# Gate and up products with both parts of x in one matmul of 512 columns, and weight sums made ahead

## The chip, the cores and the metric

One core of a Trainium2 chip runs the whole layer. The metric is the device time of one execution in microseconds (us), as the median of the runs given. A profile of one further execution stands beside it, with the granted clock of the matrix engine.

The engines are named as in the profile: PE multiplies matrices (PEld loads its weights), DVE and ACT do elementwise work, POOL and SP mostly issue DMAs. Each engine takes its own instructions strictly in the order of the program and waits for the others by semaphores.

## The reference

One encoder layer over x of 512 tokens by 2048, all in float32:

```
h = rmsnorm(x, attn_norm_w);  P = h @ w_in            # 2048 -> 6176 columns
attn = three-dilation windowed attention on P         # 16 heads of 64
gla  = bidirectional gated linear attention on P      # 4 heads
x = x + concat(attn, gla) @ w_out                     # 2048 -> 2048
h = rmsnorm(x, ffn_norm_w)
x = x + (silu(h @ w_gate) * (h @ w_up)) @ w_down      # 2048 -> 5632 -> 2048
out = rmsnorm(x, final_norm_w)
```

## The kernel before

**Precision.** A float32 operand f is used as two parts: hi, which ACT makes by casting f to the matrix engine's rounded format (fp32r), and lo = f - hi, which DVE makes. A product is the sum of three matmuls, hi by hi, hi by lo and lo by hi, which add up in PSUM. So each product costs one ACT cast and one DVE subtraction for each operand, and three PE instructions, each with a weight load of its own.

**PSUM and SBUF.** PSUM is eight banks of 512 columns (`ps`). SBUF is cut by hand into 70 slots of 512 columns (`s2`, tiles a) and 16 slots of 1024 columns (`s4`, tiles b). A slot is taken from the front of a queue and put back at its end. Whoever takes a slot waits until the last user of what stood there is through, so the order in which slots are put back decides who waits for whom. The order on every engine is the order in which this Python program emits its instructions.

**The projections.** `jobs` is a list of 24 products that `run_job` (L263) runs in turn; the first 16 are columns of w_in (twelve jobs, here by number: 0 qk0, 1 av0, 2 qk1, 3 qk2, 4 av1, 5 qk3, 6 gqk0, 7 gv0, 8 gqk1, 9 gv1, 10 gr0, 11 gr1) and four column blocks of w_out (12 to 15, out0 to out3). A job is 16 halves; a half is 128 rows of weights by 512 columns and 12 matmuls of 512 columns (L285 to L287 or L293 to L295). `Stream` (L155) loads pieces of two halves through SP, three pieces held at most, and casts and subtracts three halves ahead of use (L196, L197). After each half `run_side` runs some steps of attention or GLA, which go on in between: one step has matmuls and transposes on PE, and elementwise work that the next step's PE work needs. The evacuation of a w_out block makes the inputs of gate/up (`evac_out`, L998): transposed, weighted, and split by `pair_operands`.

**Gate and up.** The product of a 2048-row block and 256 columns of w_gate or w_up (a unit) is done by a scheme with 7 products in place of 8: with rows and columns each cut in two, R are the raw blocks and Z sums of blocks on the weight side, B and T the like on the x side. There are 44 units (22 blocks, gate and up in turn); each has four pieces of 512 rows (`seq`), and a piece two pairs p. So a piece has 2 x 7 products, and before the change 42 matmuls of 256 columns (L1147 to L1149). For a piece the kernel
- loads 512 KB through SP (`load`, L1069 on, three held at most),
- makes the four sums Z on DVE (`sums`, L1089 to L1091: one instruction of 512 columns and two of 256),
- casts (ACT, L1101: 768 columns of R, 1024 of Z) and subtracts (DVE, L1106) one piece ahead of PE (`split`),
- runs the products (`products`), which add up in four banks for a unit.

Two units fill PSUM: one is added to while the other is read. After the fourth piece `evac` (L1153) is queued in `urgent`, and one of its steps runs after each piece of the next unit (three steps for each of the first eight pieces): DVE adds the seven products into four result blocks, reading the banks themselves. Then `finish` (L1179): for a gate unit, two DVE multiplications by the row scale and a Silu on ACT; for an up unit, one DVE multiplication by the gate, and a store through POOL to `gd` in DRAM, from where the down product reads.

**After gate and up** come four small jobs of w_down, the class `Down` with the same seven-product scheme, and the final norm.

Of the kernel before, what the change touches and what calls it, by code (L numbers as in the profile page):

```python
# [117 lines left out]
def layer(nc, tc, x, attn_norm_w, w_in, rel_table, gw_f, gb_f, gw_b, gb_b, gla_norm_w, w_out,  # L118
# [7 lines left out]
    with tc.manual_schedule(), \  # L126
# [25 lines left out]
        state = {"credit": 0.0, "set": None}  # L152
# [96 lines left out]
        class Job:  # L249
            drop = None  # L250

# [11 lines left out]
        def run_job(j):  # L263
# [6 lines left out]
            for i in range(j.n):  # L270
# [690 lines left out]
        def half_split(src, n=512):  # L961

            if n == 512:
                hi, lo = s2.get(F32R), s2.get(F32R)
                return (hi, lo), hi.t, lo.t, hi.f
            o = s2.get(F32R, [P, 2, 256])
            return (o,), o.t[:, 0], o.t[:, 1], o.f[:, 0]

        def pair_operands(q, fs_):
# [10 lines left out]
            todo = []  # L980
            slots = []
            for src, n in ((f1.t[:, a], 256), (f2.t, 512), (t13.t, 512), (t24.t, 512)):
                sl, hi, lo, hf = half_split(src, n)
                slots += sl
                todo.append((src, hi, lo, hf))
            for i in range(4):
                src, hi, lo, hf = todo[i]
                act.copy(hi, src)
                sub(lo, src, hf)
                put((f1, f2, t13, t24)[i])  # L990
                if i % 2:
                    yield
            (_, b1h, b1l, _), (_, f2h, f2l, _), (_, t13h, t13l, _), (_, t24h, t24l, _) = todo
            xs[q] = dict(slots=slots, B11=(b1h, b1l), B21=(f2h[:, a], f2l[:, a]), B22=(f2h[:, z], f2l[:, z]),
                         T1=(t13h[:, a], t13l[:, a]), T3=(t13h[:, z], t13l[:, z]),
                         T2=(t24h[:, a], t24l[:, a]), T4=(t24h[:, z], t24l[:, z]))
# [62 lines left out]
        class Blocks:  # L1059
# [9 lines left out]
            def load(self):  # L1069
                while self.n_load < self.n and len(self.raw) < 3 and s4.free:  # L1070
                    w, k, n_kt, col, n = self.source(*self.seq[self.n_load])
                    r = s4.get(F32, self.shape(4))
                    sp.dma_start(out=r.t.rearrange("p a b c -> p (a b c)").rearrange("p (k c) -> p k c", k=n_kt),
                                 in_=w[k * P:(k + n_kt) * P, col:col + n].rearrange("(k p) c -> p k c", p=P))
                    self.raw[self.n_load] = r
                    self.n_load += 1

# [34 lines left out]
        class Feed(Blocks):  # L1112
# [3 lines left out]

            def __init__(self):
# [4 lines left out]
                self.begin(seq, 2, P)  # L1122

# [3 lines left out]

            def products(self, i, banks):
                st_ = self.sets.pop(i)
                piece = self.seq[i][1]  # L1130
                first, last = piece == 0, piece == self.per - 1
                a, z = slice(0, 256), slice(256, 512)
                A, B, C, E = (b.t for b in banks)
                for p in range(2):
                    q = 2 * piece + p
                    (rh, rl), (sh, sl) = st_
                    R = lambda n: (rh.t[:, p, n], rl.t[:, p, n])
                    Z = lambda n: (sh.t[:, p, n], sl.t[:, p, n])
                    x_ = xs[q]
                    prods = [(A[:, a], R(0), x_["B11"], True), (A[:, z], R(2), x_["B21"], False),  # L1140
                             (B[:, a], Z(2), x_["T2"], True), (C[:, a], Z(1), x_["T1"], True),
                             (C[:, z], Z(0), x_["T3"], False), (E[:, a], Z(3), x_["B22"], True),
                             (E[:, z], R(1), x_["T4"], False)]
                    for o, (wh, wl), (xh, xl), head in prods:
                        head = head and first and p == 0
                        end = last and p == 1
                        mm(o, wh, xh, start=head, stop=False, skip_group_check=True)  # L1147
                        mm(o, wh, xl, start=False, stop=False, skip_group_check=True)  # L1148
                        mm(o, wl, xh, start=False, stop=end, skip_group_check=True)  # L1149
# [3 lines left out]
            def evac(self, u, banks):  # L1153
# [4 lines left out]
                add = lambda o, x_, y_: dve.tensor_tensor(o, x_, y_, op=OP.add)  # L1158
                c_ = s4.get(F32, [P, 2, 512])
                c = c_.t.rearrange("p f t -> p (f t)")  # L1160
                A, B, C, E = (b.t for b in banks)
                t1, t2 = s2.get(), s2.get()
                act.copy(t1.t[:, a], A[:, a])
                add(c[:, a], A[:, z], t1.t[:, a])
                put(banks[0])
                dve.tensor_tensor(t1.t[:, z], t1.t[:, a], B[:, a], op=OP.subtract)
                yield
                add(t2.t.rearrange("p (h t) -> p h t", h=2), C.rearrange("p (h t) -> p h t", h=2),
# [112 lines left out]
        def drop_g(k):  # L1281
            put(*gT.pop(k))
# [321 lines left out]
```

## Time and profile before

| what | us |
|---|---|
| median of 3 runs | 2239.39 (2237.67 to 2239.72) |
| profiled execution, its own time | 2238.72 |
| its span in the trace | 2236.9 |
| projections of w_in with attention and GLA | 9 to 680 |
| projection of w_out | 680 to 868 |
| gate and up (first and last of its matmuls) | 868 to 1762 |
| down product and end | 1762 to 2237 |

The granted clock of PE was 0.997 over the span. A row of groups in the trace reads: line, engine, operation, what is written and what is read, shapes, count | busy time in us, mean ns of one | idle time of the engine just before them, and what ended it. A row of windows has for each stretch its length and the busy time of PE, PEld, DVE, ACT and POOL (with counts of instructions), then the granted clock, the share of time in which the 16 DMA engines were busy, and what they moved in GB/s. A row of the timeline is start, duration, engine, line. The end of a matmul is modelled: how fast matmuls follow each other is read from their starts.

### The profile page before, as it was taken

The numbers are of one execution on the slowest core, as the hardware profiler recorded it, in microseconds if no ns is written. First come the engines' busy times: TensorE is split into PE (matmuls) and PEld (weight loads), VectorE is DVE, ScalarE is ACT, GpSimd is POOL, SyncE is SP. The second block draws the span as 40 slices with busy tenths as digits, with TensorE's granted clock in tenths as the row PEclk, the third lists the DMA queues.
The fourth block names the chain that finished last, engine by engine and source line by source line (L and its number), as shares of the span: only waits on it lengthen the run. The fifth ranks groups of instructions, "written<-read, shape, count | busy, mean of one in ns | idle before, by whom it ended". The sixth has DMA issues, their size and how long they took to land.

```text
span 2236.9 us, 37003 instructions
## 1 busy us (share of the span) xinstructions
PE 2210.6 (99%) x14814; PEld 2037.6 (91%) x14814; DVE 1635.0 (73%) x2717; ACT 1002.4 (45%) x1637; POOL 115.8 (5%) x173
## 2 busy tenths in 40 slices
PE   8999999999999999999999999999999999999998
PEld 7888887888888888999999999999999999999986
DVE  4366665745454446988888888888888788888877
ACT  5344444444444344444433444344433555555542
POOL 0000000000000100000000000000000110022220
PEclk9999999999999999999999999999999999999999
DMA  5525625232324432334333333333333865688992
GB/s 205 158 75 146 181 81 142 83 123 66 95 64 143 138 125 68 113 114 124 116 123 121 114 123 114 114 123 114 123 115 116 256 179 179 171 190 185 241 368 76
DMA packets 211805, 307.78 MB, mean 138 GB/s; under 512 B 15376, under 2 KB 131264, under 8 KB 211633
## 3 DMA queue, kind: packets, MB, share of 16 engines
q1 hardware_dynamic: 192480, 259.37, 36.8%
q0 software_dynamic: 18256, 44.99, 8.5%
q8 instruction: 116, 1.90, 0.4%
q10 hardware_dynamic: 896, 1.06, 0.1%
q14 instruction: 57, 0.46, 0.1%
HBM read 246.58 MB, written 46.20 MB: 131 GB/s over the span
## 4 chain that ended last, share of the span: by engine, by line
PE 88%; issue 6%; POOL 2%; DMA 1%; DVE 1%; ACT 1%; SPq 0%; POOLq 0%; ACTq 0%; DVEq 0%
PE ps L1149 13%; PE ps L1148 13%; PE ps L1147 13%; PE ps L294 6%; PE ps L295 6%; PE ps L293 6%; PE ps L285 5%; PE ps L286 5%; PE ps L287 5%; PE ps L1376 2%; PE ps L1375 2%; PE ps L1374 2%; POOL md L1396 2%; PE ps L514 1%; PE ps L841 1%
## 5 line engine op out<-in xcount | busy, mean ns | idle before, releaser
L1149 PE MATMUL ps<-a,b 128*128 128x256 f32 x2464 | 697.7, 283 | 2.9 <-DVE b L1106 2.9
L1147 PE MATMUL ps<-a,b 128*128 128x256 f32 x2464 | 697.5, 283 | 0.0
L1148 PE MATMUL ps<-a,b 128*128 128x256 f32 x2464 | 697.3, 283 | 0.0
L1101 ACT CAST b<-b 128x768 fp32r<-128x768 f32 x480 | 445.5, 942 | 537.5 <-DVE b L1106 284.8
L1106 DVE TENSOR_TENSOR b<-b,b 128x768 fp32r<-128x768 f32 x480 | 510.2, 1089 | 139.2 <-PE ps L1148 62.5
L1149 PEld LDWEIGHTS ps<-a,b 128*128 128x128 f32 x2464 | 473.0, 192 | 3.7 <-DVE b L1106 3.7
L1148 PEld LDWEIGHTS ps<-a,b 128*128 128x128 f32 x2464 | 473.0, 192 | 0.0
L1147 PEld LDWEIGHTS ps<-a,b 128*128 128x128 f32 x2464 | 473.0, 192 | 0.0
L197 DVE TENSOR_TENSOR a<-b,a 128x512 fp32r<-128x512 f32 x292 | 195.0, 686 | 125.5 <-ACT a L196 122.8
L1376 PE MATMUL ps<-b,a 128*128 128x256 f32 x896 | 254.5, 284 | 3.6 <-DVE a L1339 3.6
L1374 PE MATMUL ps<-b,a 128*128 128x256 f32 x896 | 254.4, 284 | 1.5 <-ACT a L1338 1.5
L1375 PE MATMUL ps<-b,a 128*128 128x256 f32 x896 | 254.2, 284 | 0.0
L196 ACT CAST a<-b 128x512 fp32r<-128x512 f32 x292 | 171.3, 617 | 51.5 <-DMA b<-in_w_in_dram 18.2
L294 PE MATMUL ps<-a,a 128*128 128x512 f32 x464 | 182.0, 392 | 2.3 <-DVE a L197 2.1
L293 PE MATMUL ps<-a,a 128*128 128x512 f32 x464 | 184.1, 397 | 0.0
L295 PE MATMUL ps<-a,a 128*128 128x512 f32 x464 | 181.6, 391 | 0.0
L1376 PEld LDWEIGHTS ps<-b,a 128*128 128x128 f32 x896 | 172.7, 193 | 4.0 <-DVE a L1339 4.0
L1374 PEld LDWEIGHTS ps<-b,a 128*128 128x128 f32 x896 | 172.7, 193 | 1.7 <-ACT a L1338 1.7
L1375 PEld LDWEIGHTS ps<-b,a 128*128 128x128 f32 x896 | 172.8, 193 | 0.0
L1089 DVE TENSOR_TENSOR b<-b 128x512 f32<-128x512 f32 x240 | 164.0, 684 | 7.1 <-DMA b<-in_w_up_dram 4.1
L285 PE MATMUL ps<-a,a 128*128 128x512 f32 x416 | 168.2, 404 | 0.0
L286 PE MATMUL ps<-a,a 128*128 128x512 f32 x416 | 163.3, 392 | 0.0
(224 smaller groups left out, 3071.6 us busy)
## 6 DMA issues: line engine op xcount, KB each, us to landing
b<-in_w_gate_dram SPq DMA_DIRECT2D x88, 512.0 KB, 3.5
b<-in_w_up_dram SPq DMA_DIRECT2D x88, 512.0 KB, 3.6
b<-in_w_down_dram SPq DMA_DIRECT2D x88, 512.0 KB, 5.3
b<-in_w_in_dram SPq DMA_DIRECT2D x96, 256.0 KB, 4.5
b<-in_w_in_dram SPq DMA_DIRECT2D x48, 512.0 KB, 4.0
b<-in_w_out_dram SPq DMA_DIRECT2D x32, 512.0 KB, 4.4
md<-a POOLq DMA_DIRECT2D x56, 256.0 KB, 8.5
a<-a SPq DMA_DIRECT2D x96, 128.0 KB, 2.3
```

The lines of the kernel that those rows point to most:

```text
L285: mm(o, wh.t[:, c], xh.t, start=first, stop=False)
L293: mm(o, xh.t[:, c], wh.t[:, w], start=first, stop=False)
L294: mm(o, xh.t[:, c], wl.t[:, w], start=False, stop=False)
L295: mm(o, xl.t[:, c], wh.t[:, w], start=False, stop=last)
L1101: act.copy(hi.t, src)
L1106: dve.tensor_tensor(lo.t, src, hi.f, op=OP.subtract)
L1147: mm(o, wh, xh, start=head, stop=False, skip_group_check=True)
L1148: mm(o, wh, xl, start=False, stop=False, skip_group_check=True)
L1149: mm(o, wl, xh, start=False, stop=end, skip_group_check=True)
L1374: mm(o, xh[:, t], wh, start=first and h == 0, stop=False, skip_group_check=True)
L1375: mm(o, xh[:, t], wl, start=False, stop=False, skip_group_check=True)
L1376: mm(o, xl[:, t], wh, start=False, stop=last, skip_group_check=True)
```

## The change

It has four parts, all for gate and up.

1. **Products.** The two parts of an x operand now lie side by side in one slot of 2 x 256 columns. From unit 2 on, hi of the weights is multiplied with both parts by one matmul of 512 columns into a bank of its own, and lo of the weights with hi of x by one of 256 columns into that bank's first half. The products run product by product (both pairs of one, then the next) instead of pair by pair. Units 0 and 1 keep the three matmuls of 256 columns and four banks.
2. **Evacuation.** A unit holds seven banks. After its last piece `leave` copies all of them to SBUF on ACT, which sets the banks free; the steps of `evac` then work on the copies, and first fold the two halves of each (DVE, 256 columns).
3. **Weight sums ahead.** For 110 of the 176 pieces (all with q of 0 or 2, and q of 3 for gate units) the sums are made during jobs 1 to 14 by the generator `ahead`: SP loads the 512 KB piece, DVE makes four sums in place (four instructions of 256 columns), POOL stores the 512 KB to `sd` in DRAM. A step is one sum; `run_job` takes 1.3 steps after each half of jobs 1 to 5, 2.3 in jobs 6 to 11 and 2.9 in jobs 12 to 14. In gate and up SP then loads such a piece's sums beside its raw weights.
4. **Splits of x.** `pair_operands` makes seven casts and subtractions of 256 columns in place of one of 256 and three of 512.

```diff
@@ run_job
+                state["ahead"] += j.ahead
+                while state["ahead"] >= 1:
+                    state["ahead"] -= 1
+                    next(state["sums"], None)
             j.evac(banks)
@@ pair_operands
+            xs[q] = {}
+            for n, (name, f, h) in enumerate((("B11", f1, a), ("B21", f2, a), ("B22", f2, z), ("T1", t13, a),
+                                              ("T3", t13, z), ("T2", t24, a), ("T4", t24, z))):
+                o = xs[q][name] = s2.get(F32R, [P, 2, 256])
+                act.copy(o.t[:, 0], f.t[:, h])
+                sub(o.t[:, 1], f.t[:, h], o.f[:, 0])
...
@@ class Feed
+            PRODUCTS = (("R", 0, "B11"), ("R", 2, "B21"), ("Z", 2, "T2"), ("Z", 1, "T1"), ("Z", 0, "T3"),
+                        ("Z", 3, "B22"), ("R", 1, "T4"))
...
+                self.pre = {i: n for n, i in enumerate(i for i, (u, q) in enumerate(seq) if q != 1 and (q < 3 or u % 2 == 0))}
+                self.sd = dr.tile([len(self.pre), P, 1024], F32, name="sd")
...
+            def ahead(self):
+                todo, held = deque(self.pre), deque()
+                def load():
+                    if todo and len(held) < 2 and len(s4.free) > 1:
+                        r = s4.get(F32, self.shape(4))
+                        self.fetch(todo[0], r)
+                        held.append((todo.popleft(), r))
+                load()
+                yield
+                while todo or held:
+                    load()
+                    if not held:
+                        yield
+                        continue
+                    i, r = held.popleft()
+                    b = lambda n: r.t[:, :, n]
+                    for o, x_ in ((1, 0), (0, 2), (2, 1), (3, 2)):
+                        dve.tensor_tensor(b(o), b(o), b(x_), op=OP.add)
+                        yield
+                    pool.dma_start(out=self.sd[self.pre[i]], in_=r.t.rearrange("p a b c -> p (a b c)"))
+                    put(r)
...
+                    if i in self.pre:
+                        S = self.S[i] = s4.get(F32, self.shape(4))
+                        sp.dma_start(out=S.t.rearrange("p a b c -> p (a b c)"), in_=self.sd[self.pre[i]])
...
+            def sums(self, i):
+                if i in self.pre and i == self.n_sums:
+                    self.n_sums += 1
+                else:
+                    Blocks.sums(self, i)
@@ products
-                    for o, (wh, wl), (xh, xl), head in prods:
-                        mm(o, wh, xh, start=head, stop=False, skip_group_check=True)
-                        mm(o, wh, xl, start=False, stop=False, skip_group_check=True)
-                        mm(o, wl, xh, start=False, stop=end, skip_group_check=True)
...
+                for n, (side_, b, x) in enumerate(self.PRODUCTS):
+                    for p in range(2):
...
+                        if u > 1:
+                            o = banks[n].t
+                            mm(o, wh, x_.rearrange("p s t -> p (s t)"), start=head, stop=False, **kw)
+                            mm(o[:, 0:256], wl, xh, start=False, stop=end, **kw)
...
+            def leave(self, u, banks):
+                out_ = []
+                for n, b in enumerate(banks):
+                    e = s2.get()
+                    c = slice(0, 256 if u < 2 and n == 1 else 512)
+                    act.copy(e.t[:, c], b.t[:, c])
+                    put(b)
+                    out_.append(e)
+                return out_
@@ evac (the steps, from unit 2 on)
+                    fold = lambda *ns: [add(m[n], m[n], es[n].t[:, z]) for n in ns]
...
+                fold(0, 1, 2)
+                add(c[:, a], m[1], m[0])
+                dve.tensor_tensor(m[0], m[0], m[2], op=OP.subtract)
+                yield
+                fold(3, 4)
+                add(m[3], m[3], m[0])
+                add(c[:, 768:1024], m[3], m[4])
+                add(m[4], m[4], m[0])
+                yield
+                fold(5, 6)
+                add(c[:, 256:512], m[5], m[3])
+                add(c[:, 512:768], m[6], m[4])
+                put(*es)
+                yield
                 self.finish(u, c_, c)
@@ run
-                        banks[u] = [ps.get() for _ in range(4)]
+                        banks[u] = [ps.get() for _ in range(7 if u > 1 else 4)]
...
                     if q == self.per - 1:
-                        urgent.append(self.evac(u, banks.pop(u)))
+                        urgent.append(self.evac(u, self.leave(u, banks.pop(u))))
@@ at the end
+        state["sums"] = ff.ahead()
+        for n, j in enumerate(jobs[1:15]):
+            j.ahead = 1.3 if n < 5 else 2.3 if n < 11 else 2.9
```

More of the change, by code (lines that the diff above doesn't have):

```diff
@@ L979, in pair_operands @@
             yield
[L980 to L991, printed above, removed]
+            xs[q] = {}
[4 more added lines that the diff above has]
+                sub(o.t[:, 1], f.t[:, h], o.f[:, 0])
+                if n in (0, 2, 4, 6):
+                    put(f)
+                if n in (2, 6):
                     yield
[L993 to L996, printed above, removed]
         def evac_out(c):
@@ L1134, in products @@
[L1134 to L1143, printed above, removed]
-                    for o, (wh, wl), (xh, xl), head in prods:
[L1145 to L1149, printed above, removed]
+                (rh, rl), (sh, sl) = st_
@@ L1573, in layer @@
             if n == n_out:
+                assert next(state["sums"], None) is None
                 ff.run()
```

77 lines of the change are left out of this document (47 added, 30 removed).

## The prediction

> **What bounds the kernel now.** I read the page first: the shares of the engines and the chain of work that ended last.
>
> ```profile
> PE 2210.6 (99%) x14814; PEld 2037.6 (91%) x14814; DVE 1635.0 (73%) x2717; ACT 1002.4 (45%) x1637; POOL 115.8 (5%) x173
> DMA  5525625232324432334333333333333865688992
> GB/s 205 158 75 146 181 81 142 83 123 66 95 64 143 138 125 68 113 114 124 116 123 121 114 123 114 114 123 114 123 115 116 256 179 179 171 190 185 241 368 76
> PE 88%; issue 6%; POOL 2%; DMA 1%; DVE 1%; ACT 1%; SPq 0%; POOLq 0%; ACTq 0%; DVEq 0%
> ```
>
> PE works 99% of the span and holds 88% of the chain: what PE no longer does is won, as long as nothing else becomes late. Next come the windows by stage (job 1, jobs 2 and 3, jobs 7 and 8, out0 to out2, and all of gate/up).
>
> ```profile
> 64.50:108.02 43.52, 43.52 (x194) 36.04 (x192) 14.40 (x24) 10.71 (x20) 0.00 (x0) 1.00 0.69 203
> 108.00:228.00 120.00, 119.81 (x613) 100.39 (x612) 79.23 (x175) 57.15 (x124) 0.00 (x0) 1.00 0.38 106
> 410.30:468.70 58.40, 58.33 (x300) 48.97 (x299) 34.72 (x75) 25.55 (x54) 0.00 (x0) 1.00 0.44 134
> 468.70:522.50 53.80, 53.80 (x251) 45.12 (x250) 23.82 (x43) 22.43 (x52) 1.07 (x2) 1.00 0.26 79
> 680.20:727.20 47.00, 46.92 (x210) 38.55 (x209) 23.78 (x43) 23.14 (x51) 2.13 (x4) 1.00 0.44 146
> 727.20:774.20 47.00, 47.00 (x217) 39.08 (x217) 19.69 (x36) 17.55 (x36) 4.29 (x8) 1.00 0.40 134
> 774.20:821.20 47.00, 47.00 (x217) 39.11 (x216) 19.69 (x36) 17.86 (x36) 4.30 (x8) 1.00 0.41 135
> 868.15:1761.90 893.75, 890.82 (x7418) 889.96 (x7417) 776.86 (x1178) 370.87 (x446) 12.79 (x24) 1.00 0.39 121
> ```
>
> PE is full in all of them, at the full granted clock. DVE is busy 87% of gate/up (776.86 of 893.75), but only 33 to 66% before it. So the change takes work from PE where PE is the bound, and puts DVE and DMA work where these have room. The sum is made from what PE wins, less what each of these moves gives back.
>
> **Part 1, the matmuls.** Each matmul carries a weight load, and a short one costs more per column than a long one. The starts show it, where gate/up begins and ends:
>
> ```profile
> 868.15 0.39 PE L295 MATMUL ps<-a,b 128*128 128x512 f32 x1
> 868.38 0.28 PE L1147 MATMUL ps<-a,b 128*128 128x256 f32 x1
> 868.49 0.28 PE L1148 MATMUL ps<-a,b 128*128 128x256 f32 x1
> 868.61 0.28 PE L1149 MATMUL ps<-a,b 128*128 128x256 f32 x1
> ...
> 1761.87 0.28 PE L1149 MATMUL ps<-a,b 128*128 128x256 f32 x1
> 1761.99 0.40 PE L293 MATMUL ps<-a,a 128*128 128x512 f32 x1
> ```
>
> A matmul of 512 columns followed by one of 256 takes 0.23 us (868.15 to 868.38), and one of 256 takes 0.12 whether 256 or 512 follow (1761.87 to 1761.99). More exactly, by windows: job 1 has 192 weight loads in 43.52 us, 226.7 ns each; gate/up has 7418 matmuls in 890.82 busy us, 120.1 ns each. So 256 further columns cost 106.6 ns, and 13.5 ns come with each matmul. Three of 256 take 360.3 ns, one of 512 and one of 256 take 346.8. From unit 2 on there are 42 units x 4 pieces x 14 = 2352 such triples: 2352 x 13.5 ns = 31.8 us. Bounds: the starts at 868 leave the short one after a long one 0.11 to 0.12 us, so a pair takes 340 to 349 ns and the gain is 27 to 47 us. I take -32: it is the mean over thousands of rows.
>
> The Trainium skill, "TensorE: Matmul & The Clock Gate", section "Back-to-back issue gap", gives a warm gap of N / 2.4 + 2.5 ns, that is, only 2.5 ns that come with each matmul. By it 2352 fewer matmuls would win an estimated 6 us. The 13.5 ns of the windows above speak against it for matmuls that each load weights; what would follow is a rival below.
>
> **Part 2, does DVE or ACT become the bound of gate/up?**
>
> ```profile
> L1106 DVE TENSOR_TENSOR b<-b,b 128x1024 fp32r<-128x1024 f32 x240 | 293.3, 1222 | 17.7 <-PE ps L1148 8.5 <-ACT b L1101 6.3 <-PE ps L1376 2.9
> L1101 ACT CAST b<-b 128x1024 fp32r<-128x1024 f32 x240 | 251.9, 1049 | 222.9 <-PE ps L1148 116.5 <-PE ps L1376 55.9 <-DVE b L1106 36.0
> L1106 DVE TENSOR_TENSOR b<-b,b 128x768 fp32r<-128x768 f32 x240 | 229.3, 955 | 121.5 <-PE ps L1148 54.0 <-ACT b L1101 25.6 <-PE ps L1149 19.2
> L1101 ACT CAST b<-b 128x768 fp32r<-128x768 f32 x240 | 200.4, 835 | 314.5 <-DVE b L1106 248.8 <-PE ps L1376 24.7 <-DMA gd<-b 19.2
> L1089 DVE TENSOR_TENSOR b<-b 128x512 f32<-128x512 f32 x240 | 164.0, 684 | 7.1 <-DMA b<-in_w_up_dram 4.1 <-DMA b<-in_w_down_dram 3.0
> L1090 DVE TENSOR_TENSOR b<-b,b 128x256 f32<-128x256 f32 x240 | 102.0, 425 | 8.3
> L1158 DVE TENSOR_TENSOR a<-ps,a 128x512 f32<-128x512 f32 x44 | 30.1, 684 | 0.0
> L1184 DVE TENSOR_TENSOR b<-b,a 128x512 f32<-128x512 f32 x44 | 28.3, 684 | 0.0
> L1188 DVE TENSOR_TENSOR b<-b,b 128x1024 f32<-128x1024 f32 x22 | 26.8, 1217 | 0.0
> L1185 ACT ACTIVATE b<-b 128x1024 f32<-128x1024 f32 x22 | 23.3, 1061 | 115.8 <-DVE b L1184 110.6 <-PE ps L1149 5.2
> L1393 ACT COPY a<-ps 128x512 f32<-128x512 f32 x72 | 40.0, 589 | 14.6 <-PE ps L1376 11.6
> ```
>
> For a unit DVE now has 4 x (1222 + 955) for the splits, 4 x (684 + 2 x 425) for the sums, three adds of 256 and two of 512 columns for the evacuation (2.64 us) and 1.29 us of finishing (two of 684 or one of 1217): 18.8 us against 168 matmuls = 20.2 us. After the change the sums fall to 1.5 pieces per unit (66 of 176 over 44), and the evacuation is 14 adds of 256 columns, 425 each: 8.7 + 2.3 + 5.95 + 1.3 = 18.2 us against PE's 4 x 14 x 0.3468 = 19.4. The ratio stays, 94 for 93%, so DVE isn't the bound. ACT has 4 x (1049 + 835) + 7 x 589 + 1061 / 2 = 12.2 of 19.4 us.
>
> What does change is a queue. ACT takes the seven copies of `leave` in order, and the casts two pieces ahead stand behind them; for a gate unit a Silu stands in front of them, which waits for DVE (110.6 us of L1185's idle time is that). Take T as the start of an up unit's last piece. The casts of the next piece wait for slots that PE sets free at T (116.5 us of L1101's idle time): cast 1.05 and subtraction 1.22 end at T + 2.3, the two multiplications at T + 3.6, the Silu at T + 4.7, the first copy at T + 5.3. PE fills the spare bank first and needs the copied one at T + 4.85 (a piece) + 0.69 (one product) = T + 5.54: in time by 0.2 us. The other copies follow at 0.5 to 0.6 us, faster than the 0.69 at which PE asks, and end at T + 8.5. Then cast 0.84 and subtraction 0.96 end at T + 10.3, but PE wants that part of lo at T + 9.7 + 0.23: 0.3 to 0.4 us late, once for each gate unit's finish. 21 x 0.3 = 6 us. Bounds: 0 if the copies overlap a little more, and 1.5 us each, 32 us, if DVE is an evacuation step and a sum late when the multiplications are due. I take +6.
>
> The second DMA of a piece has its time: 6.5 loads and half a store of 512 KB in 19.4 us in place of 4 and a half in 20.2 is a share of about 0.39 x 7 / 4.5 x 20.2 / 19.4 = 0.63, with loads two and more pieces ahead (9.7 us; they land in 3.5).
>
> **Part 3, the sums made ahead.** The program order puts 19 to 22 of the 440 adds into each of jobs 1 to 5, 34 to 41 into each of jobs 6 to 11, and 45, 48 and 24 into out0 to out2. At 0.425 us each DVE rises from 66 to 81% in jobs 2 and 3 (79.23 + 41 x 0.425 = 96.7 of 120), from 59 to 89% in job 7 (34.72 + 41 x 0.425 = 52.1 of 58.4), and from 51 to 91% in out0 (23.78 + 19.1 of 47). What covers them is DVE's own idle time:
>
> ```profile
> L566 DVE CUSTOM_DVE_ANT_0 a<-ps,b 128x512 f32<-128x512 f32 x64 | 44.2, 691 | 49.2 <-PE ps L554 49.0
> L197 DVE TENSOR_TENSOR a<-b,a 128x512 fp32r<-128x512 f32 x292 | 195.0, 686 | 125.5 <-ACT a L196 122.8 <-DMA a<-in_x_dram 1.0 <-DMA b<-in_w_in_dram 1.0
> ```
>
> In attention DVE waits 0.77 us for PE in each of 64 steps (L566) and 0.43 for the cast before each split (L197); 1.3 adds are 0.55 us. In jobs 6 to 11 the step is longer, and 0.98 us of adds per half go into 1.5 to 1.9 us free (jobs 7 and 8, the stretch less DVE's busy time, over 16 halves). Steps with more of their own work than the mean will make PE wait here and there: 0 to 20 us over eleven jobs, and I take +4. If an add waits for its load, the splits and all of attention's or GLA's work queue behind it on DVE; PE has three halves (3 x 43.52 / 16 = 8 us) of split weights in hand.
>
> DMA is tighter. A piece moves 1.05 MB (load and store).
>
> ```profile
> q1 hardware_dynamic: 192480, 259.37, 36.8%
> q0 software_dynamic: 18256, 44.99, 8.5%
> b<-in_w_gate_dram SPq DMA_DIRECT2D x88, 512.0 KB, 3.5
> b<-in_w_out_dram SPq DMA_DIRECT2D x32, 512.0 KB, 4.4
> gd<-b POOLq DMA_DIRECT2D x22, 512.0 KB, 3.2
> ```
>
> Cheapest, at the 368 GB/s of the busiest slice (over 90% busy), it takes all 16 engines 2.85 us. Dearest, at the mean of the queues, 0.524 MB at 315 GB/s (259.37 MB in 36.8% of 2236.9) and 0.524 at 237 (44.99 in 8.5%), it takes 3.9. out0 and out1 carry 0.44 x 47 + 0.40 x 47 = 39.5 us now and get 12 + 11 pieces: 105 us at the cheap price, 129 at the dear one, in 94. So these two jobs become bound by DMA: +11 to +35 us, less the 8 us that PE has in hand once. The store is one run of 4 KB per partition, like `gd`'s, which lands fastest, so I stay near the cheap end: +8, range 0 to 35. out2 (19.3 + 7 x 2.85 = 39 of 47) and job 7 (25.7 + 11 x 2.85 = 57 of 58.4) just fit; SP's queue has the w_out loads behind the sums' loads, and POOL's the x loads behind the stores.
>
> **Part 4, splits of x**, are nearly free: 24 casts and 24 subtractions of 512 columns become 48 each of 256; on DVE 24 x 686 (L197) become 48 x 425 (L1090), 4 us more over the four output jobs, in which DVE is half idle. I take 0; bounds 0 to 4.
>
> **The sum**, against the profiled execution's own 2238.7: -32 + 6 + 4 + 8 = -14, so 2224.7; the median lies 0.7 higher, and I say 2225.
>
> **The rivals.**
> - Nothing is given back. For it: lateness by 0.3 us is within what such a chain can tell, and three pieces of w_out are held. 2239.4 - 32 = 2207. Against it: DMA over 100% in two jobs. Chance 0.14.
> - Slower: out0 and out1 pay the dear price, +35. For it: the mean rates of the queues; a load is asked for only one piece ahead of its add (4 / 2.9 halves of 2.94 us, 4.1 us, against 3.5 to 4.4 to land). 2239.4 - 32 + 6 + 4 + 35 = 2252. It decides from 3.6 us per piece on, 23 x 3.6 + 39.5 = 122, 28 over 94. Chance 0.20.
> - Slower: the queue on ACT. Copies, Silu and casts come 1.5 us late at each of 21 boundaries: 2239.4 - 32 + 32 + 4 + 8 = 2251. Against it: 0.2 us of room was worked out, not a lack. Chance 0.12.
> - Slower: the pair wins nothing. What comes with a matmul isn't paid for each instruction, and a pair costs what its 768 columns cost in the triple, 360.3 ns: 2239.4 + 6 + 4 + 8 = 2257. Against it: 512 columns cost 226.7 ns in job 1, not 240. Chance 0.05. The rule of the Trainium skill named above comes near this case, with 2251 as an estimate.
> - My forecast, 2214 to 2235: chance 0.45. Milder or mixed cases hold the other 0.04.
>
> **The numbers.** No change means within 0.2% (4.5 us), about what can be told: 2235 to 2244. Faster: nothing given back and nearly all of the forecast, 0.58. Slower: the three slower cases less their milder half-cases, 0.32. The rest, 0.10, is the edge between. 8 times in 10 it lies from 2205 (nothing given back) to 2254 (the dear price); the likeliest case alone is 2214 to 2235.
>
> **What would show it.** Right: 12462 matmuls; starts of a 512 and a 256 in gate/up 346 to 348 ns apart; a gate/up stage of 893.75 - 32 + 6, about 868 us, with PE's idle time there once in two units, in front of lo parts and ended by DVE, not by DMA; out0 and out1 with DMA over 90% busy, ending some 8 us later than the work before them explains; attention and GLA within a few us. Wrong: a pair of matmuls at 355 ns or more; DVE waiting for `sd` or raw loads in gate/up; idle time of PE in attention over 10 us; PE waiting for ACT's copies with every unit.

## The result, and the profile after

The changed kernel takes 2380.4 us (median of 4 runs, 2371.7 to 2381.85); the kernel before took 2238.62 beside it (4 runs, 2237.67 to 2239.72). The ratio is 1.063, with a 95% interval from 1.0615 to 1.0639: 142 us slower, where 14 us faster was forecast. The profiled execution took 2381.85 us, its span is 2380.1.

The page of the changed kernel first: the shares of the engines, the group of the new adds (L1146), and the loads of w_gate with their median time to landing.

```profile
PE 2238.4 (94%) x12462; PEld 1931.2 (81%) x12462; DVE 1743.8 (73%) x3233; ACT 1136.5 (48%) x1919; POOL 174.8 (7%) x283
...
L1146 DVE TENSOR_TENSOR b<-b 128x256 f32<-128x256 f32 x440 | 182.7, 422 | 137.9 <-DMA b<-in_w_gate_dram 83.7
...
b<-in_w_gate_dram SPq DMA_DIRECT2D x154, 512.0 KB, 4.6
```

PE has the 12462 matmuls that were forecast, and is busy longer than before all the same, 2238.4 us against 2210.6, and idle for 142 us of the span against 26. The windows say where. First those of the kernel before and after up to the first matmul of gate/up; then, of the kernel after, job 1, jobs 2 and 3, jobs 7 and 8, out0 to out2, and gate/up. Columns as in the prediction's windows.

```profile
9.00:868.00 859.00, 858.23 (x4122) 712.49 (x4123) 467.92 (x912) 382.21 (x802) 23.43 (x44) 1.00 0.39 117
```

```profile
9.00:958.00 949.00, 883.51 (x4122) 722.73 (x4123) 622.17 (x1361) 386.65 (x820) 82.25 (x154) 0.97 0.69 230
...
63.83:107.35 43.52, 43.52 (x194) 36.04 (x193) 21.05 (x43) 10.71 (x20) 2.16 (x4) 1.00 0.93 300
107.35:242.52 135.17, 124.43 (x614) 102.31 (x612) 91.42 (x214) 58.06 (x124) 5.33 (x10) 0.97 0.56 171
460.81:528.91 68.10, 61.19 (x299) 49.65 (x298) 49.86 (x117) 27.35 (x58) 5.33 (x10) 0.97 0.64 214
528.91:582.76 53.85, 53.85 (x252) 45.14 (x250) 37.37 (x80) 22.48 (x52) 5.87 (x11) 1.00 0.83 292
740.90:795.70 54.80, 53.05 (x234) 42.75 (x232) 40.67 (x87) 23.43 (x51) 5.88 (x11) 1.00 0.78 269
795.70:856.06 60.36, 49.62 (x209) 39.27 (x208) 34.78 (x82) 18.25 (x42) 10.17 (x19) 0.92 0.89 294
856.06:912.94 56.88, 47.99 (x209) 39.03 (x208) 35.16 (x79) 19.21 (x45) 11.44 (x22) 0.94 0.91 320
958.20:1901.60 943.40, 891.76 (x5065) 773.54 (x5065) 727.35 (x1232) 495.66 (x700) 12.71 (x24) 0.98 0.52 173
```

Three readings. Up to gate/up the same 4122 matmuls take 90 us more: PE is idle for 65.5 us (949.00 less 883.51; 0.8 before), and its busy time grows by 25 as the granted clock falls to 0.97. Gate/up takes 943.4 us where 893.8 stood: 51.6 us of it idle. And not every job suffers: job 1 and job 8 have DMA busy 93 and 83% of the time and PE not idle at all, while jobs 2, 3 and 7, at 56 and 64%, stall. So the share of DMA isn't what decides there.

**The loss before gate/up.** The waits of the changed kernel from 0 to 958 us (engine, line, what was waited for: us in all, times, longest), and those of SP's queue from 100 to 540 us:

```profile
DVE b L1146 <- DMA b<-in_w_gate_dram: 83.7, 24, 10.2
DVE b L1146 <- DMA b<-in_w_up_dram: 48.2, 19, 12.1
PE ps L519 <- DVE a L513: 32.2, 18, 5.2
PE ps L295 <- DVE a L197: 13.5, 7, 7.2
PE ps L288 <- DVE a L197: 10.4, 3, 6.2
...
SPq L181 <- DMA sd<-b: 86.1, 20, 9.7
SPq L1067 <- PE ps L528: 39.8, 14, 4.2
SPq L1067 <- DVE b L584: 36.2, 10, 5.9
```

DVE stands 132 us in front of the new adds (L1146) because their load hasn't landed, and behind them in its queue stand attention's scaling (L513), which PE's transposes (L519) wait for, and the splits of the streamed weights (L197). Three timelines around one such case, of DVE, of SP's queue and of PE (start, duration, engine, line; in brackets the idle time before and what ended it):

```profile
258.71 0.48 DVE L513 TENSOR_SCALAR a<-a,small 128x512 f32<-128x512 f32 x1
264.21 0.43 DVE L1146 TENSOR_TENSOR b<-b 128x256 f32<-128x256 f32 x1 [5.01 <-DMA b<-in_w_gate_dram]
...
267.71 0.49 DVE L513 TENSOR_SCALAR a<-a,small 128x512 f32<-128x512 f32 x1
```

```profile
258.09 0.60 SPq L481 DMA_DIRECT2D a<-a  x1
258.73 0.60 SPq L482 DMA_DIRECT2D a<-a  x1
259.43 0.53 SPq L1067 DMA_DIRECT2D b<-in_w_gate_dram  x1
```

```profile
262.73 0.39 PE L559 MATMUL ps<-a,a 128*128 128x512 f32 x1
268.34 1.09 PE L519 MATMUL ps<-idn,a 128*128 128x128 f32 x4 [5.22 <-DVE a L513]
```

SP issues the load only at 259.43, behind a row of attention's own copies at 0.6 us each; it lands 4.8 us later (the median of w_gate's loads over the whole run is 4.6); DVE has waited 5.01 us by then, and the next L513 ends so late that PE waits 5.22. This load was not slow. It was asked for late, in a queue that also waits for slots: the lines of SPq show the new load (L1067) waiting for slots that attention's work still uses (L528 and L584), and the weight stream (L181) waiting for a slot whose store to `sd` is on its way. From 0 to 958 us such stores are also the longest wait in front of the new load itself: 181.3 us in 32 waits.

Other loads were slow as well. The 115 loads that L1067 issues up to 958 us took 3.2 to 13.3 us to land, 5.4 in the median. An estimate from the trace: had each of the 43 that DVE waited for landed in 4.4 us (the longer of the prediction's two figures) after its own issue, some 37 of the 132 us would be gone; the rest is late asking.

**The loss in gate/up.** The waits from 958 to 1902 us:

```profile
PE ps L1186 <- ACT a L1203: 32.4, 20, 2.3
PE ps L1187 <- DVE b L1098: 17.5, 14, 2.5
DVE b L1213 <- DMA gd<-b: 49.5, 20, 4.6
```

Twenty times PE waits for the copies of `leave` (L1203), and twenty times DVE waits for a store to `gd`: about once for each of the 22 blocks. One boundary on DVE, on ACT, and on PE:

```profile
1406.06 1.22 DVE L1251 TENSOR_TENSOR b<-b,b 128x1024 f32<-128x1024 f32 x1
...
1414.79 0.43 DVE L1213 TENSOR_TENSOR b<-a,a 128x256 f32<-128x256 f32 x1 [2.98 <-DMA gd<-b]
...
1427.91 1.29 DVE L1247 TENSOR_TENSOR b<-b,a 128x512 f32<-128x512 f32 x2
```

```profile
1429.23 1.06 ACT L1248 ACTIVATE b<-b 128x1024 f32<-128x1024 f32 x1 [4.28 <-DVE b L1247]
1430.19 3.50 ACT L1203 COPY a<-ps 128x512 f32<-128x512 f32 x7
```

```profile
1428.05 0.39 PE L1186 MATMUL ps<-a,b 128*128 128x512 f32 x1
1428.28 0.28 PE L1187 MATMUL ps<-a,b 128*128 128x256 f32 x1
1430.81 0.50 PE L1186 MATMUL ps<-a,b 128*128 128x512 f32 x1 [2.25 <-ACT a L1203]
...
1432.41 0.63 PE L1186 MATMUL ps<-a,b 128*128 128x512 f32 x1
1432.83 0.41 PE L1187 MATMUL ps<-a,b 128*128 128x256 f32 x1
1433.05 0.63 PE L1186 MATMUL ps<-a,b 128*128 128x512 f32 x1
```

The up unit's result is multiplied at 1406.06 and its store to `gd` sent off at 1407.6. The gate unit's evacuation takes a 1024-column slot for its result a piece later, and gets the very slot from which that store is still going out: DVE waits 2.98 us, to 1414.79. Every later step of DVE is late by that; the gate multiplications (L1247) come at 1427.91, the Silu behind them, ACT's seven copies behind the Silu, and PE, which needs the second bank, waits 2.25 us. Then the matmuls start further apart for a while (last three lines): that is the clock, taken up at the end.

### The profile page after: what moved, and what is told of

Its sections match the earlier page's. It is cut to its first block, busy times and chain, and to the rows that moved or that the text cites. A ratio compares the mean times of both kernels' runs of the same rounds, so it can differ in the third digit from the quotient of the medians.

```text
span 2380.1 us, 33931 instructions
## 1 busy us (share of the span) xinstructions
PE 2238.4 (94%) x12462; PEld 1931.2 (81%) x12462; DVE 1743.8 (73%) x3233; ACT 1136.5 (48%) x1919; POOL 174.8 (7%) x283
## 4 chain that ended last, share of the span: by engine, by line
issue 38%; PE 28%; DVE 7%; DMA 5%; POOL 1%; ACT 1%; SPq 0%; POOLq 0%; DVEq 0%; ACTq 0%
PE ps L1447 4%; PE ps L1445 4%; PE ps L1446 4%; PE ps L1186 2%; DMA b<-in_w_gate_dram 2%; PE ps L286 2%; PE ps L288 2%; PE ps L287 2%; DMA b<-in_w_down_dram 1%; PE ps L295 1%; PE ps L296 1%; PE ps L294 1%; DVE b L1098 1%; DMA b<-in_w_up_dram 1%; PE ps L1187 1%
## 5 line engine op out<-in xcount | busy, mean ns | idle before, releaser
L1186 PE MATMUL ps<-a,b 128*128 128x512 f32 x2352 | 840.2, 400 | 32.4 <-ACT a L1203 32.4
L1187 PE MATMUL ps<-a,b 128*128 128x256 f32 x2352 | 668.4, 284 | 17.5 <-DVE b L1098 17.5
L1093 ACT CAST b<-b 128x768 fp32r<-128x768 f32 x480 | 438.6, 950 | 480.9 <-DVE b L1098 279.8
L1186 PEld LDWEIGHTS ps<-a,b 128*128 128x128 f32 x2352 | 447.8, 190 | 142.5 <-ACT a L1203 39.0
L1187 PEld LDWEIGHTS ps<-a,b 128*128 128x128 f32 x2352 | 451.0, 192 | 25.2 <-DVE b L1098 25.2
L1146 DVE TENSOR_TENSOR b<-b 128x256 f32<-128x256 f32 x440 | 182.7, 422 | 137.9 <-DMA b<-in_w_gate_dram 83.7
L197 DVE TENSOR_TENSOR a<-b,a 128x512 fp32r<-128x512 f32 x292 | 198.1, 685 | 56.7 <-ACT a L196 56.7
L295 PE MATMUL ps<-a,a 128*128 128x512 f32 x464 | 184.9, 399 | 12.3 <-DVE a L197 12.1
L294 PE MATMUL ps<-a,a 128*128 128x512 f32 x464 | 186.4, 402 | 0.0
L296 PE MATMUL ps<-a,a 128*128 128x512 f32 x464 | 182.9, 394 | 0.0
L288 PE MATMUL ps<-a,a 128*128 128x512 f32 x416 | 165.7, 398 | 10.4 <-DVE a L197 10.4
L286 PE MATMUL ps<-a,a 128*128 128x512 f32 x416 | 170.2, 409 | 0.0
L287 PE MATMUL ps<-a,a 128*128 128x512 f32 x416 | 165.0, 397 | 0.0
L1203 ACT COPY a<-ps 128x512 f32<-128x512 f32 (+1 forms) x302 | 155.3, 599 | 8.3 <-PE ps L1193 4.1
```

Source lines behind the costliest of these rows:

```text
L286: mm(o, wh.t[:, c], xh.t, start=first, stop=False)
L287: mm(o, wh.t[:, c], xl.t, start=False, stop=False)
L288: mm(o, wl.t[:, c], xh.t, start=False, stop=last)
L294: mm(o, xh.t[:, c], wh.t[:, w], start=first, stop=False)
L295: mm(o, xh.t[:, c], wl.t[:, w], start=False, stop=False)
L1093: act.copy(hi.t, src)
```

## The experiments

Each ran as one execution beside one of the kernel before on the same chip (2238.46 us for e1 to e5, 2238.50 for e6, e7, e8 and e11), but e9, e10, e12 and e13, which ran several times. "Start" is the first matmul of gate/up (868.4 before, 958.25 after), "stage" the time from its first to its last matmul (893.5 and 943.2, by the starts). How far a start can be trusted is seen from e1 and e8, which do the same work up to there and start at 868.0 and 869.8.

### e1_no_ahead: no sums ahead of gate/up

```diff
-self.pre = {i: n for n, i in enumerate(i for i, (u, q) in enumerate(seq) if q != 1 and ...)}
+self.pre = {}
```

> The changed kernel without its part 3: no weight sums made ahead, no loads or stores for them, all four sums of each piece made by DVE within gate/up. Theory 1 (the 90 us lost before gate/up come from the sums made ahead alone): gate/up starts at 868 us as in the kernel before, not at 958. In gate/up DVE gets 4 pieces of sums for a unit in place of 1.5, 22 us by its own durations against 19.4 of PE, so that stage becomes bound by DVE, 890 to 940 us. Total 2235 to 2285. Rival (the splits of x or the 512-column products cost in the projections too): gate/up starts later than 880 us.

Measured: 2327.94 us; start 868.0, stage 977.1. So all of the loss before gate/up belongs to the sums ahead. Within gate/up, DVE has all sums to make, and PE waits 59.8 us in front of the copies (20 times, up to 3.2 us), 27 more than in the changed kernel: without the sums ahead the same boundary is later still. But the reason is another, for DVE waits for no store to `gd` there; it is late by its own work.

### e3, e4, e5: the boundary in gate/up

e3 takes the result slot (`c_`) at the unit's last piece, ahead of the steps that put the other unit's slot back; e4 issues the copies ahead of those steps, so that no Silu stands in front of them; e5 does both.

```diff
+if q == self.per - 1:
+    es, c_ = self.leave(u, banks.pop(u)), s4.get(F32, [P, 2, 512])
...
-urgent.append(self.evac(u, self.leave(u, banks.pop(u))))
+urgent.append(self.evac(u, es, c_))
```

> The changed kernel, with the result slot of a unit's evacuation taken before the finish of the unit before puts its own slot back; the order on ACT stays. Theory A (the stalls in gate/up start with DVE, which waits 20 times, 49.5 us in all, for the store to gd to land, because the evacuation of a gate unit gets the slot that is just being stored): that wait goes to under 5 us, the waits of PE for banks (32 us) and for lo parts (17 us) fall by more than half, gate/up (944 us from first to last matmul) comes to 880 to 900, total 2315 to 2340. Theory B (the Silu in front of the copies on ACT is enough to make the banks late): PE still waits over 25 us for banks, total over 2350.

> The changed kernel, with the seven copies of leave emitted ahead of the last evacuation step of the unit before, so that no Silu stands in front of them on ACT; the slot stays as it is. Theory B: the waits for banks go from 32 to under 5 us, total about 2335 to 2350. Theory A: banks are free in time, but DVE still waits 49 us for the store, the lo parts come late (17 us or more), and of the 80 us of stalls in gate/up more than 30 remain.

> Both edits of the two runs before. If A and B are both part of it: no wait of DVE for the store, none of PE for banks over 3 us in all, gate/up 868 to 878 us from first to last matmul, as forecast for that stage, and total 2305 to 2318, the rest of the loss being what lies before gate/up (90 us). If it is above 890 us, something else holds the stage.

Measured: e3 2322.56, e4 2312.28, e5 2309.62 us, with stages of 884.5, 876.1 and 876.1. What PE still waited for in e3's gate/up:

```profile
PE ps L1186 <- ACT a L1203: 2.4, 6, 0.4
...
PE ps L1187 <- DVE b L1098: 0.4, 1, 0.4
```

With the slot alone, DVE's 49.5 us of waiting for `gd` are gone, and PE's 49.9 us shrink to 2.8: the chain read above is the cause, and the stage loses 58.7 of the 67.1 us that lie between the changed kernel and e5. The other 8.4 go only when no Silu stands in front of the copies. e4 leaves DVE waiting for `gd` (12.4 us, 20 times) and PE doesn't notice; it is faster than either theory had it. So the wait for the store harms only through the queue on ACT, and the order there alone cures all of it. The starts stay at 955 to 960, so the two losses are separate.

### e6, e11, e7: what the sums ahead cost before gate/up

e6 keeps loads and stores and leaves the adds out. e11 makes 440 adds at the same places on one scratch slot, without loads (e1 otherwise). e7 gives the adds to POOL.

```diff
-                        dve.tensor_tensor(b(o), b(o), b(x_), op=OP.add)   # e6: left out
+                        pool.tensor_tensor(b(o), b(o), b(x_), op=OP.add)  # e7
...
+                dve.tensor_tensor(scratch, scratch, scratch, op=OP.add)   # e11: 440 of these
```

> The changed kernel with the 440 adds of the sums made ahead left out; loads and stores stay, so raw weights go to DRAM in place of sums and the result is not the layer's. Theory P (DVE waits in its queue for loads that come late, 132 us in all, and attention and the splits behind it come late): without the adds nothing on DVE waits, gate/up starts at 868 to 885 us instead of 958. Theory Q (the traffic itself: SP's queue, where 86 us of waits of w_in loads are for a store to land, or the DMA engines): gate/up starts after 920 us all the same.

> The kernel of e1 (no sums ahead, all sums in gate/up) with 440 adds of 256 columns on a scratch tile at the places where the sums ahead stood, without loads or stores: DVE's time alone, no waits. If the time of the adds is the cost, gate/up starts at 930 to 960 us as with the real ones; if DVE's idle time covers them, as the prediction had it, at 868 to 875 us, and the total is that of e1, 2328, plus that.

> The changed kernel with the 440 adds made by POOL, which has nothing else in that stage but DMA issues; loads and stores as before. Theory P: DVE no longer waits for these loads, gate/up starts at 868 to 895 us; the rest of the loss, 50 us in gate/up, stays: total 2290 to 2325. Theory Q: over 920 us to the start of gate/up, total over 2345. If POOL is so slow that its sums come late, PE does not wait for them before gate/up, but slots come free later, which would lie between.

Measured, by the start of gate/up: e6 869.6, e11 875.3, e7 917.8 (2290.2, 2336.73 and 2336.33 us in all; e11's stage is 980.4, as e1's). Against e1's 868.0 the adds' time alone costs 7 us and both together on DVE 90; the 1.6 of the traffic alone can't be told from nothing, as e8 starts at 869.8 without any. In e6 SP waits for attention's slots as in the changed kernel (from 100 to 540 us):

```profile
SPq L1067 <- PE ps L528: 43.1, 13, 6.0
SPq L1067 <- DVE b L584: 42.2, 13, 6.1
```

85 us of waiting in front of the same loads, which land later still (6.1 us in the median), and no harm, since nothing on DVE waits for them. The cost is neither the work nor the traffic, but that an add stands in DVE's queue while its load is late. e7 takes the wait to an idle engine and wins 40 of the 90 back, not all: a POOL add takes 846 ns against DVE's 422, PE still waits 20.3 us for L513 (19.5 of them at once) and 11.9 for the splits behind ACT's casts. The one long wait, in the waits of ACT and of PE from 0 to 918 us:

```profile
ACT b L583 <- DMA sd<-b: 20.9, 1, 20.9
PE ps L519 <- DVE a L513: 20.3, 2, 19.5
```

A cast of attention (L583) got a slot from which a store to `sd` was still to go out, and DVE and PE stood behind it: pieces held longer keep slots from attention. So with the adds on POOL the slots are a second way for the same traffic to do harm. How much of the other loss in e7 comes from slots wasn't tested alone.

### e8_no_ahead_both: no sums ahead, the boundary cured

> Wide products and copies without sums ahead, with the copies in front of the Silu and the result slot taken early. DVE then has about 22 us of work by its durations for a unit of 19.4 us. With the overlap of 0.08 us that neighbouring instructions show it is 20.4. If DVE is the bound, gate/up is 885 to 905 us, total 2228 to 2250, no better than the kernel before; if it is 870 to 880, DVE was never the bound, and the total comes to 2213 to 2224.

The edits of e1 and e5 together. Measured: 2269.51 us; start 869.8, stage 921.5. The window from 900 to 1700 us:

```profile
900.00:1700.00 800.00, 778.58 (x4356) 661.88 (x4356) 767.01 (x1351) 428.30 (x594) 10.11 (x19) 1.00 0.37 114
```

DVE is busy 96% and is the bound; PE waits 21.2 us for its subtractions (69 times), and the stage is longer than the 885 to 905 us that were expected of a DVE bound. So the sums do have to leave gate/up, in part at least: folding the banks took what DVE had free.

### e9_pool_sums, e12_pool_all: POOL makes sums in gate/up

e9 has e5's edits and nothing ahead; POOL makes the sums of the 110 pieces in gate/up. In e12 POOL makes them for all pieces from unit 1 on.

```diff
-            def sums(self, i):
+            def sums(self, i, eng=dve):
...
+                Blocks.sums(self, i, pool if i in self.pre else dve)
```

> Wide products; copies in front of the Silu and the slot early; nothing made ahead: the sums of the 110 pieces are made by POOL within gate/up (846 ns for 256 columns in the run with adds on POOL, so about 3.3 us a piece and 8 us of each 19.4 us unit), the other 66 by DVE. If DVE is relieved as by the sums ahead and POOL does not slow it: gate/up starts at 868 to 870, lasts 876 as with both edits, total 2219 to 2226, faster than the kernel before by 0.5 to 0.9%. If POOL and DVE hinder each other in SBUF, DVE's durations rise above 1222 ns for a subtraction of 1024 columns and the total passes 2235.

> As the run with the sums on POOL, but POOL makes all sums from unit 1 on: about 13 us of POOL and 15 of DVE for a unit of 19.4 us. If PE's own rate is all that is left, gate/up comes to 868 to 876 us and the total to 2214 to 2224, at most 8 us better than with 110 pieces on POOL; if POOL is late with a sum (four in a row, no slack for the casts), slower than that run by up to 30 us.

Measured: e9 2347.7 us (ratio 1.049, 1.0471 to 1.0506; stage 1003.0), e12 2381.25 (1.064, 1.0621 to 1.0653; 1032.5). Groups by form, of e9 from 900 to 1700 us and of e5 from 980 to 1780 us (the fold is L1207 in the one, L1213 in the other):

```profile
L1207 DVE TENSOR_TENSOR a<-a 128x256 f32<-128x256 f32 x233 | 182.2, 827 | 0.0
L1240 DVE TENSOR_TENSOR b<-b,a 128x512 f32<-128x512 f32 x36 | 52.7, 1503 | 0.0
L1081 POOL TENSOR_TENSOR b<-b 128x512 f32<-128x512 f32 x88 | 166.3, 1889 | 297.0 <-DVE b L1098 277.9 <-PE ps L1187 11.8 <-DMA b<-in_w_gate_dram 4.8
```

```profile
L1213 DVE TENSOR_TENSOR a<-a 128x256 f32<-128x256 f32 x269 | 99.8, 419 | 0.0
L1246 DVE TENSOR_TENSOR b<-b,a 128x512 f32<-128x512 f32 x40 | 25.7, 684 | 0.0
```

The same fold takes DVE 827 ns in place of 419, the same multiplication 1503 in place of 684, when POOL adds in the same stage. Within e9, the 103 folds of that group with no POOL addition beside them take 416 ns in the mean, the 130 with one 1152; so it is POOL's work beside them that makes them slow. PE waits 89.3 us for DVE's subtractions (61 times). Work moved to POOL isn't taken off DVE here.

### e10_part_ahead, e13_late_ahead: fewer sums ahead, in jobs that don't stall

Both have e5's edits and make the sums of one piece of four ahead (44 pieces, 176 adds). e10 runs 1.3 steps per half in job 1 and 2.6 in jobs 8 to 11; e13 2.8 in jobs 8 to 11 alone, which the adds of the changed kernel had hardly made longer (53.9, 52.6, 51.3 and 54.2 us by their first matmuls, for 53.8, 52.6, 51.3 and 53.7 before).

```diff
-self.pre = {... if q != 1 and (q < 3 or u % 2 == 0)}
+self.pre = {... if q == 1}
...
-        for n, j in enumerate(jobs[1:15]):
-            j.ahead = 1.3 if n < 5 else 2.3 if n < 11 else 2.9
+        for j in jobs[8:12]:
+            j.ahead = 2.8
```

> Wide products, both edits, and only 44 sums ahead (q of 1 of each unit), in job 1 at 1.3 steps a half and in jobs 8 to 11 at 2.6, none while attention or the w_out blocks run. Theory P with few slots (the loads come late only where attention or the GLA outputs hold most of the 16 slots): jobs 8 to 11 stay at 211 to 214 us together and gate/up starts at 868 to 872. If it is DMA traffic, the denser adds stretch jobs 8 to 11 by over 8 us. Gate/up with 3 pieces of sums for a unit lies between the 876 with 1.5 and the 921 with 4, about 885 to 900; total 2228 to 2250.

> As the run with 44 sums ahead, but all of them in jobs 8 to 11, at 2.8 steps a half, so that no slot is held and no step is taken while attention runs. If the 6 us that gate/up still started late there (874 against 868) come from the slots held through attention and the few adds there, jobs 2 to 7 return to the times of the kernel before and gate/up starts at 868 to 871, total 2224 to 2229 (0.994 to 0.996 of before). If they come from the sums in jobs 8 to 11, those jobs grow and the total stays at 2231 or more.

Measured: e10 2231.7 us (7 runs; ratio 0.997, 0.9959 to 0.9981; start 874.3, stage 878.8), e13 2225.26 (5 runs, 2223.17 to 2226.24, against 2237.83; ratio 0.994, 0.9928 to 0.9955; start 870.1, stage 874.6). e13 beats both kernels, the one before by 0.6%. Its span is 15.0 us shorter than that of before (2221.9 against 2236.9): gate/up gives 18.9, the stretch up to it costs 1.7, the end 2.1. e10 starts gate/up 2 us later than was expected: jobs 2 to 7 take 0.7 to 0.9 us more each, though no add runs in them. `ahead`, once begun in job 1, holds its loaded pieces in slots through them, which would explain it; in e13, where it begins in job 8, they are back at the times of before.

## Why the prediction was wrong, by its own steps

The measured terms beside the forecast ones, by e5 and the starts: the matmuls -17.4 (forecast -32), the queue on ACT +67.1 (+6), the stretch before gate/up with the sums ahead and their traffic +89.9 (+4 and +8), and 3.5 after gate/up, which no run explains; together 143, as the spans differ (2380.1 against 2236.9). What failed is that two waits were put at nearly nothing: that of DVE's queue behind late loads, and that for a slot whose store is on its way.

- **The matmuls, -32.** Right in kind and sign, too large. Where nothing stalls (e5, e13) gate/up gives 17 to 19 us. The forecast's 346.8 ns for a pair is exact in one of two rhythms that PE keeps (346.7 measured), but in the other a pair takes 353.3, and e5 stays in that one throughout. e13 has 445 pairs of the one to 1895 of the other, 352.5 in the mean; against the 360 of three short ones that is 7.5 x 2352 = 18 us. The bounds of 340 to 349 came from starts at the edge of two stages and left the second rhythm out. The rival "the pair wins nothing" is ruled out by the same runs. The gap of N / 2.4 + 2.5 ns in the Trainium skill, "TensorE: Matmul & The Clock Gate", section "Back-to-back issue gap", which the prediction set beside its own figure, is given there for an isolated matmul, and the section says that in a stream of weight loads and matmuls both set the spacing. Here one matmul fewer wins 6.7 or 13.3 ns (360.0 less 353.3 or 346.7), not 2.5.
- **The queue on ACT, +6.** The place was right, the size was not: 49.9 us of waits for ACT's copies and DVE's subtractions, and gate/up as a whole 49.7 longer; e5, without these waits, has the stage 67.1 us shorter. The forecast put 1.5 us for each boundary in case "DVE is an evacuation step and a sum late when the multiplications are due", and gave it 0.12. That is what happened, and the reason was left out of the working. The evacuation has four steps in place of three, so the up unit puts its slot back a piece later, and the loads of sums hold further slots; the front of the queue is then the slot just put back with its store on the way, and that store lands 7.1 us after its issue at 1407.6, where 3.2 was the median before. e3 shows the wait by curing it. e1, with the four steps but without the loads of sums, has no wait for `gd`; the two parts weren't tested apart. The prediction's own lines held a hint: the 19.2 us that ACT's casts of 768 columns waited for `gd` (18 times, 1.1 us at most) say that whoever came next got such a slot before too, where it did no harm. The chain of times from T was worked out with DVE free to start.
- **The sums in the jobs, +4.** This step failed most. It set the adds' time against DVE's mean idle time, which is nearly right for the time alone (e11: 7), and saw that DVE's queue would stand still behind a late load. But it judged the loads by "4.1 us, against 3.5 to 4.4 to land", counted from the issue. SP came to issue late, behind attention's copies and behind slots that were still held, and the loads then took 5.4 us in the median. The 43 waits of DVE are 3.1 us in the mean and 12.1 at most, so most of them, taken singly, are shorter than the 8 us of split weights that PE has in hand. But those weights are no store for L513, on which attention's next step on PE hangs: PE waits 32.2 us for it, and 23.9 for the splits. Some 61 of the 90 us fall in jobs 2 to 7.
- **DMA in out0 and out1, +8, and the rival with +35.** The output jobs lose 29 us together, near the dear case: out0 takes 54.8, out1 60.4 and out2 56.9, for 52.3, 45.3 and 45.3 before, by their first matmuls. But only out1 and out2 show DMA at 89 to 91%, and e6, with all the traffic, starts gate/up at 869.6. There DMA is 99 and 101% busy from 730 to 780 and from 780 to 830 us, and out0 to out2 take 52.2, 45.3 and 45.3 us, as before. So DMA's rate was not the bound; the same waiting adds were.
- **DVE as the bound** was weighed at 94 to 93% and held off rightly for the change as it stands, though the size was off: DVE is busy 727 of 943 us (77%), and 83% of the stage in e5, where nothing stalls. The sum of durations counts twice what neighbouring instructions overlap: the trace has an L1227 of 0.43 us starting at 1415.25, and the next instruction starts at 1415.59. e8 shows how near it is: without the sums ahead it is 96% busy and sets the time.
- **The splits of x, 0**, took nothing that any run could show.
- **The signs to look for.** Of the four that would show the forecast wrong, one came in full, PE idle in attention over 10 us, and one in half, PE waiting for copies with every second unit; DVE did wait for raw loads, but ahead of gate/up and not in it. That e13's 2225.26 us equals the forecast is chance: its terms are others.

## What to carry to other kernels

Before giving an idle engine more work, ask what that work waits for: 183 us of adds cost 7, and their traffic nothing that could be told, but adds in an in-order queue behind late loads cost 90, since everything behind them waited too. Count a load's lead from the moment its queue comes to issue it, with the slot it needs free. And when a change puts a slot of a shared queue back later, or holds more of them, look up who takes that slot next and what is still reading it: moving one `get` ahead of a few lines took 59 us out of a stage.

## What the runs showed of the hardware

**Two rhythms of one stream of matmuls.** Pairs of a 512- and a 256-column matmul, each with its own weights, run in e13 in one of two steady patterns with no wait in either and the granted clock at 1.00: starts 347, 347, 346 ns apart, or 350, 361, 349. Windows of e13 (the first and last in the longer one, the second in the shorter):

```profile
1100.00:1300.00 200.00, 200.00 (x1133) 173.48 (x1132) 189.22 (x330) 112.85 (x155) 2.66 (x5) 1.00 0.46 149
1435.00:1535.00 100.00, 100.00 (x578) 88.20 (x578) 96.89 (x170) 56.91 (x79) 1.60 (x3) 1.00 0.47 153
1600.00:1700.00 100.00, 100.00 (x568) 86.67 (x568) 95.39 (x165) 56.56 (x78) 1.60 (x3) 1.00 0.48 153
```

578 matmuls in 100 us against 568. The pattern changed in e13 only where the stream had been interrupted, at 1421 to 1426 and at 1582 us, and held for hundreds of pairs in between. What chooses it stays open; kept in the shorter one, gate/up would be some 1895 x 6.6 ns = 12.5 us shorter than in e13.

**Stalls cost clock too.** The changed kernel's trace has 21 stretches at a granted clock of 0.5, mostly 3.4 us long (3 in the trace before), 47.8 us of them before gate/up and 30.7 in it. A pair takes 640 ns in them (1432.41 to 1433.05 above) where it takes 347 at the full rate, so 0.46 of that time is lost where PE works all through it: at most some 22 us of the 90, and 14 us in gate/up. The boundary shown above, by windows:

```profile
1428.30:1432.00 3.70, 1.45 (x9) 1.05 (x8) 0.90 (x2) 2.77 (x5) 0.00 (x0) 1.00 0.76 271
1432.00:1435.40 3.40, 3.40 (x14) 2.87 (x13) 0.95 (x2) 3.37 (x6) 0.00 (x0) 0.53 0.00 0
```

The half rate follows a wait of 2.25 us. The Trainium skill, "TensorE: Matmul & The Clock Gate", section "Part 1: The HAM clock gate", has the array fall to half its clock after an idle window of about 3.4 us. The length agrees; but here 3.70 us with PE busy for 1.45 of them were enough.

**POOL and DVE hinder each other.** 419 to 827 ns for a fold and 684 to 1503 for a multiplication in e9, above, and within e9 416 ns for a fold alone and 1152 beside a POOL addition. The Trainium skill, "SBUF — State Buffer", section "SBUF: two separate sides", says that a DVE instruction with two SBUF inputs and a GpSimd instruction that reads SBUF exclude each other for the whole instruction. The rows fit that: a fold beside an addition is longer by 0.7 us in the mean, where POOL's additions take 0.9 to 1.9 us.
